# Left-over attention columns split with the first tile, a later product in the retention, row sums of the last down-projection on VectorE

## The chip, the cores and the metric

The kernel runs on one NeuronCore of a Trainium2 chip. A core has five engines with an instruction queue each: TensorE (PE; its weight loads are shown apart as PEld), VectorE (DVE), ScalarE (ACT), GpSimd (POOL) and SyncE (SP), which here issues the DMAs. Each runs its queue in order and waits on semaphores for the others. The metric is the device time in microseconds of one execution; lower is better.

## The reference, cut to what matters

The kernel computes one layer of a hybrid encoder in float32: an input projection, stick-breaking attention beside multi-scale retention, an output projection, and a gated feed-forward block with a causal convolution. Three places matter here.

Attention of the prompt: 8 heads of 64, keys 0 to 2063 (16 meta tokens and 2048 frames), each query reading the keys before it:

```python
z = jnp.einsum('bhqd,bhkd->bhqk', q, k) * (SB_HEAD_DIM ** -0.5)
log_1m = jnp.where(mask, jax.nn.log_sigmoid(-z), 0.0)
later = lax.cumsum(log_1m, axis=z.ndim - 1, reverse=True) - log_1m
a = jnp.where(mask, jnp.exp(jax.nn.log_sigmoid(z) + later), 0.0)
return jnp.einsum('bhqk,bhkd->bhqd', a, v)
```

Retention: the output of each head is normalised by its own root mean square and multiplied by a gate:

```python
ret = _head_norm(ret_o, g_ret_out, RET_HEADS) * jax.nn.silu(r_g)
```

Feed-forward: `u = h @ w_up`, a convolution of width 3 along the tokens, `f = (silu(gate) * val) @ w_down`, the residual sum, and a last RMS norm.

## The kernel before, in words

A float32 product is made of two halves: ACT rounds a tile to its high part and another engine subtracts that from the tile to get the low part; PE then multiplies high by high, high by low and low by high. The profile shows these pairs as `wh`/`wl` and `fh`/`fl` (lines 102 and 103), and as `ahi`/`alo` in the attention (1117 and 1118).

**Attention.** The program runs through the projection and the attention of the sample rows first (to 425 us), then through the prompt's attention (425 to 1275 us). There the work is cut into units: 256 queries (two tiles of 128) by up to 512 keys, for one head. A unit has three stages, written two or three units apart: scores and their sigmoids (L1095 to 1098, ACT L889), with the running products along the keys (DVE scan L899) and their multiplication into the weights on POOL (L905); `t()`, in which PE transposes the weights block by block into two PSUM tiles `tt`, one for each query tile (L1124, L1127), and the helper `evac` splits what is there into `ahi` (ACT) and `alo` (DVE, in0 the PSUM tile, in1 `ahi`); and `av()`, the product with the values (L1157). The PSUM pool of `tt` has two buffers, so that the transposes of the next unit wait until both splits of this one have been read. 2064 keys are 16 blocks of 128 and 16 more; so the last unit of each pair of query tiles and head, 64 units in all, has 16 columns left over (`rem`), which are transposed as two more blocks, one for each query tile, into the first PSUM tile. Such a unit has three splits: the blocks of tile 0, the left-over columns of both, the blocks of tile 1.

**Retention.** `interleave` lays the steps of the retention between those of the attention by estimated PE time. The retention goes through 17 token tiles for each of 4 heads; each has eight steps of projection (`k` 0 to 7, three matmuls `dm` each, L798 to 800), and between them stand the steps of `tail()` of the two tiles before: `prev` and `prev2`. What the table in the loop says for `prev2` is, in order: products with the state, the norm factor `rs` on POOL (L95, L97), `mt` = oc x rs x gate on DVE (L783), and the store of `mt`. The tile `gate` has two buffers; ACT writes it first (L717) when the eight steps of its tile are through, and that buffer is the one which `mt` of two tiles before reads.

**Last down-projection.** The second half of the tokens is multiplied with `w_down` by a Strassen-like scheme of seven products P1, P5, P2, P6, P4, P7, P3, eleven steps (`NH`) each: 77 steps `n` of nine matmuls (three token tiles by three halves, L1816 to 1818). The left operands are quarters of `f`, loaded from DRAM; `sum_part` makes the sums of quarters that P5, P6, P7 and P3 need, 44 in all, on POOL (L1399 to 1405), at steps that the table `when` gives. `split_part` makes `fh` and `fl` two steps ahead, and `part()` goes on with splitting the weights; per step DVE makes one `fl` and one `wl`. `taken` adds a finished product from PSUM into the output tiles `y` (DVE L1732 from PSUM, POOL L1732 from the tile `t`). In the steps n < 4 the last convolution of the up-projection is worked off (DVE L1456 and L1464, POOL L1462), two steps of it for each n.

## Time and profile before

| | |
|---|---|
| time, median of 3 runs | 3021.35 us (3019.08 to 3021.6) |
| the profiled execution's own time | 3019.77 us |
| its span | 3018.0 us, mean granted clock 0.993 |
| busy: PE, PEld | 2920.7 us (97%), 2600.2 us (86%) |
| busy: DVE, ACT, POOL | 2176.0 (72%), 1569.4 (52%), 1648.1 us (55%) |
| DMA | 535.15 MB, mean 177 GB/s |

"Busy" is time in which an engine executes; what a row shows in brackets, as `[2.36 <-DVE alo L1118]`, is the idle time of the engine right before that row and the instruction that ended it. Time outside the span (1.8 us) is start and end of the program.

### The profile page before, as it was taken

Reading aid. Unit: us, or ns where it says so; the run is one execution under the profiler, and the core shown is the slowest. Engines: PE = TensorE matmul, PEld = TensorE weight load, DVE = VectorE, ACT = ScalarE, POOL = GpSimd, SP = SyncE. Lnnn points to the kernel's source line nnn. Section 1 sums busy time; section 2 is a strip of 40 time slices with the busy share of each in tenths; the row PEclk is TensorE's granted clock in tenths of the full one; section 3 lists DMA queues with packets and bytes.
Section 4 is the critical chain, followed back from the end, with each engine's and each line's share of the span. In section 5 each row is a group of like instructions: output and inputs, shape, how many; then the busy total and the mean of one; then the engine's idle time right before and its main releaser. Section 6 shows DMA issues by size and latency. Waiting matters only on the chain. (4 is left out here: it accounts for less than half of the span.)

```text
span 3018.0 us, 48868 instructions
## 1 busy us (share of the span) xinstructions
PE 2920.7 (97%) x16735; PEld 2600.2 (86%) x16735; DVE 2176.0 (72%) x3061; ACT 1569.4 (52%) x3532; POOL 1648.1 (55%) x1826
## 2 busy tenths in 40 slices
PE   7999999999999999999999999999999999999998
PEld 6888688788888878877899998789998879999776
DVE  4331359888888888844348887778888667888897
ACT  5332467777777777643334344454444444444554
POOL 1220368788788878843335565434446343444455
PEclk9999999999999999999999999999999999999999
DMA  6865763443343443258658986655445655444662
GB/s 221 286 213 174 271 195 105 127 133 106 126 147 106 124 138 99 83 205 266 188 180 264 285 278 232 195 168 153 150 149 166 229 187 165 149 149 149 220 220 93
DMA packets 295780, 535.15 MB, mean 177 GB/s; under 512 B 38548, under 2 KB 125972, under 8 KB 283628
## 3 DMA queue, kind: packets, MB, share of 16 engines
q1 hardware_dynamic: 295532, 532.03, 54.2%
q8 instruction: 133, 2.18, 0.3%
q14 instruction: 115, 0.94, 0.1%
HBM read 383.16 MB, written 148.62 MB: 176 GB/s over the span
## 5 line engine op out<-in xcount | busy, mean ns | idle before, releaser
L905 POOL TENSOR_TENSOR sp<-sp,pr 128x272 f32<-128x272 f32 (+7 forms) x453 | 482.5, 1086 | 170.2 <-DVE pr L899 54.8
L103 POOL TENSOR_TENSOR wl<-raw,wh 128x512 fp32r<-128x512 f32 x220 | 325.8, 1482 | 377.6 <-ACT wh L102 358.0
L102 ACT ACTIVATE wh<-raw 128x512 fp32r<-128x512 f32 x561 | 342.6, 623 | 211.6 <-DMA raw<-d_ws 147.0
L1548 PE MATMUL mm<-xs,wl 128*128 128x384 f32 x1232 | 411.5, 334 | 0.0
L1547 PE MATMUL mm<-xs,wh 128*128 128x384 f32 x1232 | 411.5, 334 | 0.0
L1546 PE MATMUL mm<-xs,wh 128*128 128x384 f32 x1232 | 411.5, 334 | 0.0
L899 DVE TENSOR_TENSOR_SCAN pr<-sn,pr 128x513 f32<-128x513 f32 (+2 forms) x320 | 363.1, 1173 | 29.8 <-ACT sn L889 23.8
L1456 DVE SCALAR_TENSOR_TENSOR c<-u,cw,c 128x768 f32<-128x768 f32 (+1 forms) x264 | 343.8, 1302 | 2.5 <-POOL u L1450 1.3
L103 DVE TENSOR_TENSOR wl<-raw,wh 128x512 fp32r<-128x512 f32 x341 | 268.0, 786 | 18.1 <-ACT wh L102 17.6
L1462 POOL TENSOR_TENSOR c<-u,c 128x768 f32<-128x768 f32 (+1 forms) x66 | 116.4, 1764 | 269.7 <-ACT u L1461 264.7
L1118 DVE TENSOR_TENSOR alo<-tt,ahi 128x256 fp32r<-128x256 f32 (+3 forms) x496 | 217.1, 473 | 56.5 <-ACT ahi L1117 55.5
L798 PE MATMUL dm<-wh,xt 128*128 128x512 f32 (+1 forms) x544 | 244.2, 449 | 4.9 <-ACT vtok L459 2.6
L1117 ACT ACTIVATE ahi<-tt 128x256 fp32r<-128x256 f32 (+3 forms) x496 | 194.1, 442 | 91.5 <-DVE alo L1118 66.7
L1546 PEld LDWEIGHTS mm<-xs,wh 128*128 128x128 f32 x1232 | 231.3, 188 | 0.1
L1547 PEld LDWEIGHTS mm<-xs,wh 128*128 128x128 f32 x1232 | 231.3, 188 | 0.1
L1548 PEld LDWEIGHTS mm<-xs,wl 128*128 128x128 f32 x1232 | 231.3, 188 | 0.0
L800 PE MATMUL dm<-wh,xt 128*128 128x512 f32 (+1 forms) x544 | 215.6, 396 | 0.0
L799 PE MATMUL dm<-wl,xt 128*128 128x512 f32 (+1 forms) x544 | 215.1, 395 | 0.0
L889 ACT ACTIVATE sn<-z 128x512 f32<-128x512 f32 (+2 forms) x360 | 169.4, 471 | 80.5 <-PE z L1096 28.1
L1506 PE MATMUL mm<-xt,wh 128*128 128x298 f32 x704 | 204.2, 301 | 0.0
L1505 PE MATMUL mm<-xt,wh 128*128 128x298 f32 x704 | 203.3, 301 | 0.0
L1124 PE MATMUL tt<-ident,sp 128*128 128x128 f32 x1088 | 170.7, 274 | 27.6 <-DVE alo L1118 22.3
(285 smaller groups left out, 8052.0 us busy)
## 6 DMA issues: line engine op xcount, KB each, us to landing
xt<-d_xt SPq DMA_DIRECT2D x68, 1024.0 KB
raw<-in_wup SPq DMA_DIRECT2D x220, 256.0 KB
raw<-d_ws SPq DMA_DIRECT2D x176, 256.0 KB
raw<-in_wdn SPq DMA_DIRECT2D x121, 256.0 KB
d_ws<-raw SPq DMA_DIRECT2D x88, 256.0 KB
d_xt<-xt SPq DMA_DIRECT2D x17, 1024.0 KB
d_f<-c SPq DMA_DIRECT2D x44, 384.0 KB
fr<-d_f SPq DMA_DIRECT2D x44, 384.0 KB
```

What stands on the lines that cost most here:

```text
L102: S.activation(out=hi, in_=raw, func=AF.Copy)
L103: lo_engine.tensor_tensor(out=lo, in0=raw, in1=hi.bitcast(F32), op=ALU.subtract)
L798: PE.matmul(ps[:r], lhsT=xt[:, 0, k, :r], rhs=wh, start=k == 0, stop=False)
L799: PE.matmul(ps[:r], lhsT=xt[:, 0, k, :r], rhs=wl, start=False, stop=False)
L800: PE.matmul(ps[:r], lhsT=xt[:, 1, k, :r], rhs=wh, start=False, stop=k == KD - 1)
L899: V.tensor_tensor_scan(out=pr[:, j, s:n + 1], data0=sn[:, j, s:n + 1], data1=sn[:, j, s:n + 1], initial=1.0 if carry is None else carry[:, ...
L905: G.tensor_tensor(out=sp[:, j, c], in0=sp[:, j, c], in1=pr[:, j, c], op=ALU.mult)
L1118: V.tensor_tensor(out=lo[d], in0=x, in1=hi[d].bitcast(F32), op=ALU.subtract)
L1456: V.scalar_tensor_tensor(out=cvs[e][:, :W], in0=u[:, 2 - y:W + 2 - y], scalar=cw[:, ch, y:y + 1], in1=cvs[e][:, :W], op0=ALU.mult, op1=ALU ...
L1546: PE.matmul(ps, lhsT=wh[:, w], rhs=x[:, 0], start=k == 0, stop=False)
L1547: PE.matmul(ps, lhsT=wh[:, w], rhs=x[:, 1], start=False, stop=False)
L1548: PE.matmul(ps, lhsT=wl[:, w], rhs=x[:, 0], start=False, stop=k == 3)
```

## The change

1. `t()`: the transposed left-over columns of both query tiles are split together with the blocks of tile 0, as one piece of `nb + 2` blocks; so two splits for such a unit in place of three, and `av()` takes the last block's two halves from `src[:, 0, nb:nb + 2]`. 64 splits on ACT and 64 on DVE fall away, and the same columns are covered.
2. Retention: the step of `prev2` with `mt` goes from k = 4 to k = 5, and the one with its store from k = 5 to k = 6.
3. Last down-projection: the sums of quarters go from POOL to DVE, each in the step three before its use; the quarters' buffers are opened at n = 0, on the pool stack's right side, and their loads begin at n = 2 in place of 4; `y11` and `y21` are loaded elsewhere; the convolution goes over ten steps, one piece each; products are taken from k = 3 on. After P6, POOL adds `tmp` into `y12`, `y21` and `y22`; P7 then goes from PSUM straight into `y21` and `y22` by DVE. POOL's adds stay nine. PE's instructions keep their order in the whole program.

```diff
--- before.py
+++ after.py
@@ -798,7 +798,7 @@
                     PE.matmul(ps[:r], lhsT=xt[:, 0, k, :r], rhs=wh, start=k == 0, stop=False)
                     PE.matmul(ps[:r], lhsT=xt[:, 0, k, :r], rhs=wl, start=False, stop=False)
                     PE.matmul(ps[:r], lhsT=xt[:, 1, k, :r], rhs=wh, start=False, stop=k == KD - 1)
-                    for who in {0: (prev,), 1: (prev2,), 2: (prev2,), 4: (prev, prev2), 5: (prev2,), 6: (prev,)}.get(k, ()):
+                    for who in {0: (prev,), 1: (prev2,), 2: (prev2,), 4: (prev,), 5: (prev2,), 6: (prev, prev2)}.get(k, ()):
                         next(who, None)
                     if h + 1 < RH and ((i == 0 and 1 <= k < 7) or (1 <= i <= 2 and k == 4)):
                         part()
@@ -1129,10 +1129,10 @@
                         if u is not None:
                             for x in range(2):
                                 PE.transpose(tp[:, nb + x], u.os[:, 128 * x:128 * x + 128], ident)
-                        if nb > off:
-                            evac((slice(None), j, slice(off, nb)), tp[:, off:nb])
-                        if rem and j == 0:
-                            evac((slice(None), slice(None), nb), tp[:, nb:nb + 2])
+
+                        to = nb + 2 if rem and j == 0 else nb
+                        if to > off:
+                            evac((slice(None), j, slice(off, to)), tp[:, off:to])
                         if u is not None:
                             u.finish(tp[:, nb:nb + 2])
                     yield 220 * nb + (440 if rem else 0)
@@ -1154,7 +1154,8 @@
                         end = self.c == self.nch - 1 and x == len(seq) - 1
                         vs = vt[:, b0 + b, 128 * e:128 * e + 128]
                         for z, src in enumerate((self.hi, self.lo)):
-                            PE.matmul(o[:, :w], lhsT=vs, rhs=src[:, 0:w // 128, b], start=first and z == 0, stop=end and z == 1)
+                            rhs = src[:, 0, b:b + 2] if b == self.nb else src[:, 0:w // 128, b]
+                            PE.matmul(o[:, :w], lhsT=vs, rhs=rhs, start=first and z == 0, stop=end and z == 1)
                         if x % 2 == 1:
                             yield 440
                     if self.c == self.nch - 1:
@@ -1396,13 +1397,13 @@
                 q = {x: t[:, k] for x, t in quarters.items()}
                 name = DOWN_PRODUCTS[j][0]
                 if name == "P5":
-                    G.tensor_tensor(out=q["s"], in0=q["21"], in1=q["22"], op=ALU.add)
+                    V.tensor_tensor(out=q["s"], in0=q["21"], in1=q["22"], op=ALU.add)
                 elif name == "P6":
-                    G.tensor_tensor(out=q["s"], in0=q["s"], in1=q["11"], op=ALU.subtract)
+                    V.tensor_tensor(out=q["s"], in0=q["s"], in1=q["11"], op=ALU.subtract)
                 elif name == "P7":
-                    G.tensor_tensor(out=q["21"], in0=q["11"], in1=q["21"], op=ALU.subtract)
+                    V.tensor_tensor(out=q["21"], in0=q["11"], in1=q["21"], op=ALU.subtract)
                 elif name == "P3":
-                    G.tensor_tensor(out=q["s"], in0=q["12"], in1=q["s"], op=ALU.subtract)
+                    V.tensor_tensor(out=q["s"], in0=q["12"], in1=q["s"], op=ALU.subtract)
 
         def split_part(b, n):
             if n < 7 * NH:
@@ -1713,6 +1714,12 @@
                     if x >= 1:
                         out_of(x - 1)
 
+        def opened_quarters():
+            stb.close()
+            fp = pool(std, "p4fq", 1, "right")
+            for q in ("21", "22", "12", "s"):
+                quarters[q] = fp.tile([128, NH, WB // 2], F32, name=f"f{q}")
+
         def down_fast(opened, b, W, last_conv, gfin):
 
             tiles = blocks[b]
@@ -1773,14 +1780,13 @@
                 elif name == "P6":
                     V.tensor_tensor(out=tmp[x], in0=ps, in1=tmp[x], op=ALU.add)
                     yield
-                    add("12", x, tmp[x], G)
+                    for q in ("12", "21", "22"):
+                        add(q, x, tmp[x], G)
                 elif name == "P4":
                     add("21", x, ps)
                 elif name == "P7":
-                    V.tensor_tensor(out=tmp[x], in0=ps, in1=tmp[x], op=ALU.add)
-                    yield
-                    add("21", x, tmp[x], G)
-                    add("22", x, tmp[x], G)
+                    add("21", x, ps)
+                    add("22", x, ps)
                     yield
                     square("21", x)
                     scaled("21", x)
@@ -1794,18 +1800,10 @@
                     finish(1, x)
                 yield
 
-            loads = [(4 + k, q, k) for k in range(NH) for q in ("21", "22")]
-            loads += [(4 + NH + k, "12", k) for k in range(NH)]
-            loads += [(NH - 2 + x, "y11", x) for x in range(nt)] + [(2 * NH - 4 + x, "y12", x) for x in range(nt)]
-            loads += [(2 * NH - 2 + x, "y22", x) for x in range(nt)] + [(4 * NH + x, "y21", x) for x in range(nt)]
-
-            when = {}
-            for n in range(NH, 2 * NH):
-                when.setdefault(n - 3, []).append(n)
-            at = 2 * NH - 2
-            for n in list(range(3 * NH, 4 * NH)) + list(range(5 * NH, 7 * NH)):
-                when.setdefault(min(int(at), n - 3), []).append(n)
-                at += 1.6
+            loads = [(2 + k, q, k) for k in range(NH) for q in ("21", "22")]
+            loads += [(NH + 4 + k, "12", k) for k in range(NH)]
+            loads += [(NH + x, "y11", x) for x in range(nt)] + [(2 * NH - 4 + x, "y12", x) for x in range(nt)]
+            loads += [(2 * NH - 2 + x, "y22", x) for x in range(nt)] + [(3 * NH + x, "y21", x) for x in range(nt)]
             taking = []
             for j, (name, _) in enumerate(DOWN_PRODUCTS):
                 pss = [pm.tile([128, 512], F32, name="mm", tag="mm") for _ in range(nt)]
@@ -1820,7 +1818,9 @@
                 held = []
                 for k in range(NH):
                     n = j * NH + k
-                    if n == 4:
+                    if n == 0:
+                        opened_quarters()
+                    if n == NH - 1:
                         for _ in last_conv:
                             pass
                         pl = opened()
@@ -1829,8 +1829,7 @@
                             load_y(q[1:], kk)
                         else:
                             load_quarter(b, q, kk, W)
-                    for x in when.get(n, ()):
-                        sum_part(x)
+                    sum_part(n + 3)
                     split_part(b, n + 2)
                     part()
                     ops = (*parts.pop(n), *wts.pop(("e", b, j, k)))
@@ -1839,12 +1838,11 @@
                         continue
                     for x in range(nt):
                         products(x, k, ops)
-                        if not n and x == 0:
+                        if x == n == 0:
                             next(last_conv, None)
-                    if n < 4:
+                    if n < NH - 1:
                         next(last_conv, None)
-                        next(last_conv, None)
-                    for _ in range((k > 0) + (j == 6)):
+                    for _ in range((k > 2) + (j == 6)):
                         if taking:
                             t = taking.pop(0)
                             if next(t, 1) is None:
@@ -1894,10 +1892,6 @@
                     stx.close()
                     p4["xb"] = pool(stb, "p4xb", 1, "right")
                 if fast:
-                    stb.close()
-                    fp = pool(std, "p4fq", 1)
-                    for q in ("21", "22", "12", "s"):
-                        quarters[q] = fp.tile([128, NH, W // 2], F32, name=f"f{q}")
                     return pool(std, "p4y", 3)
                 pl = pool(std, "p4y", 6)
                 if b + 1 == len(blocks):
```

The order on DVE around one such unit of the attention, before (`pr` is the scan of one query tile, `alo` the low half of a split, `mt` the product of the retention, `scm` its masked scores, `ob` the output of a finished head):

```order
L899 SCALAR_TENSOR_TENSOR pr<-sn_2686,pr 128x513 x2
L783 SCALAR_TENSOR_TENSOR mt<-oc,rs,gate 128x128
L1118 TENSOR_TENSOR alo<-tt,ahi 128x256
L1118 TENSOR_TENSOR alo<-tt,ahi 128x2x128
L1118 TENSOR_TENSOR alo<-tt,ahi 128x128
L1173 TENSOR_REDUCE ob<-tt 128x2x64
L754 TENSOR_TENSOR scm<-rs,tri_t 128x128
```

and now:

```order
L899 SCALAR_TENSOR_TENSOR pr<-sn_2686,pr 128x513 x2
L1118 TENSOR_TENSOR alo<-tt,ahi 128x512
L1118 TENSOR_TENSOR alo<-tt,ahi 128x128
L1174 TENSOR_REDUCE ob<-tt 128x2x64
L783 SCALAR_TENSOR_TENSOR mt<-oc,rs,gate 128x128
L754 TENSOR_TENSOR scm<-rs,tri_t 128x128
L899 SCALAR_TENSOR_TENSOR pr<-sn_2687,pr 128x513 x2
```

`mt` stood ahead of the unit's splits and stands behind them, and three `alo` are two.

The order on POOL in the last down-projection, before, from the last piece of the convolution to the last sum (`fs`, `f` are quarters and their sums; `y<-t,y` adds a taken product, `y<-y,gfin` scales an output tile):

```order
L1462 TENSOR_TENSOR c<-u,c 128x768
L1399 TENSOR_TENSOR fs<-f_32487,f_32488 128x384 x11
L1401 TENSOR_TENSOR fs<-fs,f_28785 128x384 x11
...
L1405 TENSOR_TENSOR fs<-f_32489,fs 128x384 x9
L1732 TENSOR_TENSOR y<-t,y 128x512 x4
L1405 TENSOR_TENSOR fs<-f_32489,fs 128x384
L1732 TENSOR_TENSOR y<-t,y 128x512 x2
L1757 TENSOR_TENSOR y<-y,gfin 128x512 x3
L1405 TENSOR_TENSOR fs<-f_32489,fs 128x384
```

and now:

```order
L1463 TENSOR_TENSOR c<-u,c 128x768
L1764 TENSOR_TENSOR y<-y,gfin 128x512 x3
L1739 TENSOR_TENSOR y<-t,y 128x512 x9
L1764 TENSOR_TENSOR y<-y,gfin 128x512 x3
L1751 TENSOR_TENSOR ss<-ss 128x1
```

No sum of quarters is left in POOL's queue; the nine adds stand together.

The order on DVE at the start of the last down-projection, before (`c` are pieces of the convolution):

```order
L103 TENSOR_TENSOR wl<-raw,wh 128x512
L1456 SCALAR_TENSOR_TENSOR c<-u,cw,c 128x768 x2
L103 TENSOR_TENSOR fl<-f_28785,fh 128x384
L103 TENSOR_TENSOR wl<-raw,wh 128x512
L1456 SCALAR_TENSOR_TENSOR c<-u,cw,c 128x768 x2
L103 TENSOR_TENSOR fl<-f_28785,fh 128x384
L103 TENSOR_TENSOR wl<-raw,wh 128x512
L1464 TENSOR_TENSOR c<-c 128x768
```

and now, from the same place on to the first sum:

```order
L1457 SCALAR_TENSOR_TENSOR c<-u,cw,c 128x768 x2
...
L1457 SCALAR_TENSOR_TENSOR c<-u,cw,c 128x768
L103 TENSOR_TENSOR fl<-f_28657,fh 128x384
L103 TENSOR_TENSOR wl<-raw,wh 128x512
L1457 SCALAR_TENSOR_TENSOR c<-u,cw,c 128x768
...
L1465 TENSOR_TENSOR c<-c 128x768
...
L1400 TENSOR_TENSOR fs<-f_32268,f_32269 128x384
L103 TENSOR_TENSOR fl<-f_28657,fh 128x384
L103 TENSOR_TENSOR wl<-raw,wh 128x512
```

The second pair of pieces is taken apart, and one sum stands in each step from there on.

## Rows read from the trace of the kernel before

**Rows 1.** Two stretches of the program: the stretch and its length, then the busy us (and instructions) of PE, PEld, DVE, ACT and POOL, the granted clock, the DMA share and GB/s.

```profile
425.00:1275.00 850.00, 817.45 (x5424) 716.34 (x5423) 741.78 (x1281) 621.09 (x1810) 700.27 (x830) 1.00 0.37 121
...
2826.00:3018.00 192.00, 168.39 (x699) 130.57 (x697) 160.03 (x195) 94.26 (x187) 92.21 (x83) 0.97 0.54 180
```

**Rows 2.** Who waited for whom in 425 to 1275 us: total us, times, longest us.

```profile
ACT ahi L1117 <- DVE alo L1118: 63.1, 63, 4.1
DVE alo L1118 <- ACT ahi L1117: 53.4, 103, 2.0
...
DVE mt L783 <- POOL rs L97: 29.6, 29, 2.7
...
PE tt L1124 <- DVE alo L1118: 20.5, 22, 2.4
```

**Rows 3.** Groups of instructions by line and shape in 425 to 1275 us: number, busy us, mean ns, idle time before them.

```profile
L798 PE MATMUL dm<-wh,xt 128*128 128x512 f32 x414 | 180.9, 437 | 0.0
L1118 DVE TENSOR_TENSOR alo<-tt,ahi 128x256 fp32r<-128x256 f32 x306 | 118.6, 415 | 52.1 <-ACT ahi L1117 51.4
L1118 DVE TENSOR_TENSOR alo<-tt,ahi 128x512 fp32r<-128x512 f32 x116 | 74.5, 674 | 2.2 <-ACT ahi L1117 1.9
L783 DVE SCALAR_TENSOR_TENSOR mt<-oc,rs,gate 128x128 f32<-128x128 f32 x51 | 36.9, 724 | 27.6 <-POOL rs L97 27.6
```

**Rows 4.** The timeline (start, duration, instruction, idle time before it) around one unit with left-over columns: three rows of DVE, one of ACT, one of PE.

```profile
643.83 1.36 DVE L783 SCALAR_TENSOR_TENSOR mt<-oc,rs,gate 128x128 f32<-128x128 f32 x1 [0.38 <-POOL rs L97]
645.12 0.41 DVE L1118 TENSOR_TENSOR alo<-tt,ahi 128x256 fp32r<-128x256 f32 x1
645.98 0.62 DVE L1118 TENSOR_TENSOR alo<-tt,ahi 128x256 fp32r<-128x256 f32 x2 [0.45 <-ACT ahi L1117]
645.56 0.55 ACT L1117 ACTIVATE ahi<-tt 128x256 fp32r<-128x256 f32 x2 [2.75 <-DVE alo L1118]
646.55 0.63 PE L1124 MATMUL tt<-ident,sp 128*128 128x128 f32 x4 [1.35 <-DVE alo L1118]
```

**Rows 5.** The timeline around a stall of PE elsewhere: two rows of DVE, one of PE.

```profile
548.60 0.35 DVE L783 SCALAR_TENSOR_TENSOR mt<-oc,rs,gate 128x128 f32<-128x128 f32 x1 [1.31 <-POOL rs L97]
550.84 0.60 DVE L1118 TENSOR_TENSOR alo<-tt,ahi 128x256 fp32r<-128x256 f32 x2
551.39 0.85 PE L1124 MATMUL tt<-ident,sp 128*128 128x128 f32 x6 [1.00 <-DVE alo L1118]
```

**Rows 6.** ACT's split of a quarter in two neighbouring steps of the last down-projection.

```profile
2962.82 0.53 ACT L102 ACTIVATE fh<-f 128x384 fp32r<-128x384 f32 x1 [1.01 <-issue]
2964.88 0.53 ACT L102 ACTIVATE fh<-f 128x384 fp32r<-128x384 f32 x1 [1.01 <-issue]
```

**Rows 7.** Seven stretches of the last down-projection, columns as in Rows 1.

```profile
2826.00:2847.00 21.00, 14.32 (x56) 9.51 (x55) 17.66 (x28) 12.05 (x22) 5.68 (x6) 1.00 0.63 216
2847.00:2875.00 28.00, 28.00 (x124) 22.98 (x123) 24.62 (x31) 14.69 (x28) 13.32 (x12) 1.00 0.99 336
2875.00:2899.00 24.00, 21.99 (x87) 15.42 (x87) 24.00 (x27) 11.23 (x22) 15.75 (x12) 1.00 0.83 297
...
2920.00:2931.00 11.00, 9.42 (x38) 6.47 (x37) 10.94 (x10) 6.38 (x14) 9.13 (x7) 1.00 0.34 107
2931.00:2959.00 28.00, 27.74 (x122) 22.42 (x120) 28.00 (x30) 14.50 (x28) 21.12 (x15) 1.00 0.45 142
2959.00:2994.00 35.00, 34.98 (x153) 28.66 (x153) 30.67 (x40) 18.22 (x40) 13.08 (x9) 1.00 0.23 66
2994.00:3007.00 13.00, 8.29 (x26) 6.06 (x25) 4.86 (x8) 3.40 (x6) 6.64 (x12) 0.74 0.33 122
```

**Rows 8.** DVE at the start of the last down-projection, with the convolution's pieces.

```profile
2836.78 2.07 DVE L1456 SCALAR_TENSOR_TENSOR c<-u,cw,c 128x768 f32<-128x768 f32 x2
...
2844.82 0.96 DVE L1464 TENSOR_TENSOR c<-c 128x768 f32<-128x768 f32 x1 [1.85 <-POOL c L1462]
```

**Rows 9.** DVE's splits with POOL quiet (2898 us) and with POOL at its sums (2926 us).

```profile
2898.49 0.55 DVE L103 TENSOR_TENSOR fl<-f,fh 128x384 fp32r<-128x384 f32 x1
2898.96 0.68 DVE L103 TENSOR_TENSOR wl<-raw,wh 128x512 fp32r<-128x512 f32 x1
...
2925.47 1.37 DVE L103 TENSOR_TENSOR fl<-fs,fh 128x384 fp32r<-128x384 f32 x1
2926.76 1.49 DVE L103 TENSOR_TENSOR wl<-raw,wh 128x512 fp32r<-128x512 f32 x1
```

**Rows 10.** POOL's sums for P6, POOL's last sum, and PE at the end.

```profile
2874.42 14.90 POOL L1401 TENSOR_TENSOR fs<-fs,f 128x384 f32<-128x384 f32 x11
2996.16 1.00 POOL L1405 TENSOR_TENSOR fs<-f,fs 128x384 f32<-128x384 f32 x1
3000.91 0.79 PE L1816 MATMUL mm<-wh,fh 128*128 128x512 f32 x1 [3.93 <-ACT fh L102]
```

**Rows 11.** Groups by line and shape in 2825 to 3018 us, as in Rows 3: one of PE, three of POOL.

```profile
L1816 PE MATMUL mm<-wh,fh 128*128 128x512 f32 x231 | 91.6, 397 | 5.3 <-ACT fh L102 5.3
L1405 POOL TENSOR_TENSOR fs<-f,fs 128x384 f32<-128x384 f32 x11 | 14.8, 1376 | 0.0
L1732 POOL TENSOR_TENSOR y<-t,y 128x512 f32<-128x512 f32 x9 | 13.7, 1540 | 30.7 <-DVE t L1780 22.4 <-DVE t L1774 8.3
L1399 POOL TENSOR_TENSOR fs<-f,f 128x384 f32<-128x384 f32 x11 | 12.8, 1162 | 16.9 <-DMA f<-d_f 16.9
```

## The prediction

> **What bounds the kernel now.** I read the busy times by stretch first [rows 1]. The two stretches that the change touches differ. In the attention (850 us) PE is busy 817.45 us, so 32.6 us of it are open; DVE is busy 741.78 us, or 87%, and POOL 700.27. In the last down-projection (192 us) PE is open for 23.6 us, DVE is busy 160.03 and POOL only 92.21. Ahead of 2826 us the change touches nothing but the attention and the retention beside it. PE sets the pace in both; the question is which of its open microseconds end with something that the change shortens.
>
> For the attention the waits say it [rows 2]. PE's largest wait is the transpose `tt` for `alo`: 20.5 us in 22 times. That is the PSUM tile that is not yet read. Behind it stand ACT waiting for `alo` (63.1 us, 63 times), DVE waiting for `ahi` (53.4, 103 times) and `mt` waiting for `rs` (29.6, 29 times). The timeline shows how they hang together [rows 4]: `mt` waits 0.38 us for POOL and runs 1.36; the first `alo` of the unit begins only at 645.12; ACT has been waiting 2.75 us for it; then the last `alo` waits 0.45 for ACT, and PE, idle for 1.35 us, goes on at 646.55. The second place [rows 5] has no left-over columns: `mt` waits 1.31 us, `alo` comes late by that, PE loses 1.00.
>
> For the last down-projection I set matmuls against time. ACT's rows stand 2.06 us apart [rows 6], so nine matmuls take 2.06 and one 0.229. Each stretch's count times 0.229, taken from its length, is what is lost there [rows 7]: 8.2 us in 2826 to 2847 (56 matmuls, 12.8 of 21), none to 2875, 4.1 to 2899 (87), 2.3 in 2920 to 2931 (38), 0.1 to 2959, none to 2994 (153 x 0.229 = 35.0), 7.05 in 2994 to 3007 (26). Together 21.8 us.
>
> **The change part by part.** Two splits for three: two pieces of 256 cost DVE 2 x 415 ns, one of 512 674 [rows 3]. That is 156 ns, x 64 = 10 us of DVE, and the third split's idle 0.45 us x 64 = 29 us more of its time [rows 4]. None of it is on the path by itself, since DVE's work hides beside PE; it counts where PE waits for `alo`. Merged, the first split begins later, behind two more transposes, and ends 0.26 us later; but the first PSUM tile was held for the second of the three splits anyway, so its release is no later than before. ACT's second wait, for DVE to be done with the first piece, goes.
>
> `mt` one step later: 414 `dm` triples lie in 850 us [rows 3], so a step is 2.05 us, and the mean wait of `mt` is 29.6 / 29 = 1.02 [rows 2]. Most of the waits go; those of 2.1 to 2.7 stay in part. So DVE gets back up to some 28 us of standing. The store of `mt` moves by as much and stays one step behind it on SP's queue, so that nothing behind it is held longer. POOL's `rs` does not become earlier; only DVE no longer stands for it.
>
> What PE gets of this: the 20.5 us, and a little more, since a matmul that lasts 0.397 us [rows 11] is followed after 0.229 when nothing waits, so each stall costs up to 0.17 beyond the idle shown, 22 x 0.17 = 3.7. Of these 24 us both causes together cover most, but behind DVE the scans remain (DVE would still have some 732 us of work in 850). I take 17. The ends: nothing, if each stall has a second cause that comes up at once (the next is PE's own order and POOL's products); and 33 us plus 5 of restarts, if all of PE's open time goes.
>
> The start of the down-projection: a pair of pieces of the convolution is 2.07 us on DVE [rows 8], beside 0.55 + 0.68 of splits, 3.3 a step where PE needs 2.06. Now most steps hold one piece, 0.55 + 0.68 + 1.04 = 2.27, less the overlap of neighbouring rows (0.55 long, but 0.47 apart [rows 9]), about 2.05. One pair still stands. I take 2.5 of the 8.2 us (one pair's excess of 1.0, and most of the 1.85 for POOL's piece, which now has steps in between).
>
> The sums on DVE: no row shows one. The nearest is `fl`, the same shape, two inputs from SBUF: 0.55 with POOL quiet, 1.37 beside POOL [rows 9]; POOL itself takes 1.16 to 1.38 [rows 11]. I take 0.55, because POOL has no sums left to run beside it: 0.55 + 0.68 + 0.55 = 1.78, below 2.06. So 44 sums cost PE nothing. The upper end, 1.38, makes a step 2.61, or 2.37 with three overlaps of 0.08, and 44 x 0.31 = 14 us of loss. Below nothing it cannot go.
>
> What leaves with POOL's sums: beside its 14.90 us of P6 sums [rows 10] DVE's splits took 1.37 and 1.49, that is 2.8 a step instead of 1.2, and PE lost 4.1 us there and, beside P7's, 2.3 and 0.1 [rows 7]. These 6.5 go. At the end `fh` waited for the last sum, issued behind POOL's adds at 2996.16, and PE lost 3.93 in one piece [rows 10], then ran at 0.74 of its clock [rows 7], that is partly at 1.2 in place of 2.4 GHz, having stood idle before; of the 7.05 us I take 6.5. What is new: nine adds of 1.54 us stand together after P6 [rows 10, 11], 13.9 us in which DVE's two splits need some 2.7 a step, five steps with 0.65 too much, 3.3 us, less what the two steps of lead take up; I take 1.5. P7 costs DVE six adds for three before, two or three us in steps that have room. The quarters come two steps sooner; DMA is full at 0.99 from 2847 to 2875 [rows 7] and POOL's first sums waited 16.9 us for it [rows 11]. On DVE such a wait would hold `fl`; six steps lie between load and use, 12 us, and I take nothing for it.
>
> Sum: 2.5 + 6.5 + 6.5 - 1.5 = 14 for the down-projection, 17 for the attention, 31. The profiled execution took 3019.77, 1.8 more than its span and 1.6 less than the median; from it 31 give 2988.8, from the median 2990.4. I say 2989.
>
> **The rivals.** *The attention gains nothing.* PE's 817 us and POOL's 700 would set the pace, and a removed stall would be waited for elsewhere, in `alo` behind the scans. For it: DVE would still be 732 / 850 = 86% busy, POOL 82%. Against it: the waits of PE name `alo`, and both rows that I followed end in pieces that go. 3021 - 14 = 3007.
>
> *The sums are as dear on DVE as on POOL.* 1.38 each: loss 14, so the down-projection gains nothing, 3021 - 17 = 3004. Against it: `fl` at 0.55. The same time comes out if DVE waits for quarters, about 14 us in all. The Trainium skill ("Perfetto Trace Analysis", Optimizing Scalar/DVE Operations) speaks for this one: VectorE and GpSimd share a read port, so shifting operations between the two might not help. The rows at 0.55 and 1.37 agree that the two disturb each other, yet they also show that the disturbance ends when POOL is quiet, which it becomes.
>
> *All stalls of the attention go*, 38 us, and the down-projection's 14 beside: 3021 - 52 = 2969, or some 2973 if part of the restarts stays.
>
> *Slower: the gate.* `mt` reads the `gate` buffer that ACT refills at the end of step 7. From step 4 there were three steps, 6.1 us; from step 5 there are two, 4.1. If DVE lags behind ACT by more, ACT stands at L717 and with it the sigmoids and `ahi` queued behind, for which POOL and PE wait. The longest wait of ACT for DVE is 4.1 us [rows 2], so it decides just there. With 51 products in the stretch [rows 3], 2 us each and half of it on PE: 51 us lost, less 14: 3058; with 1 us each 3032, which I take as its time. Against it: the mean lag is far smaller, 63.1 / 63 = 1.0 us [rows 2].
>
> *Nothing in sum*, gains of one part eaten by the other: 3021.
>
> **How the numbers follow.** My forecast 0.50, own range 2976 to 3002 (attention 7 to 27, down-projection 12 to 18). No gain in the attention 0.16, dear sums 0.12, all stalls gone 0.10, the gate 0.06, nothing 0.06. The range 2973 to 3010 holds the forecast and most of the first three rivals. 0.2%, about 6 us, is what a measurement of this kernel can tell from no change: faster is the forecast (0.50), all stalls gone (0.10) and the two at 3004 and 3007 (0.28), less 0.01, so 0.87; the same is the last case, 0.06; slower is the gate with that 0.01, 0.07.
>
> **What would show it.** The two splits: rows of `alo` 128x512 rise by about 64, PE's wait for `alo` falls from 20.5 to below 8, DVE's for `ahi` to about 25. `mt` waits for `rs` less than 8 us in all. The attention ends by 1258 rather than 1275. In the down-projection DVE's sums take 0.55, `fl` stays at 0.55 nearly everywhere, PE's wait of 3.93 at the end is gone, and it lasts about 178 us. I am wrong if ACT's `gate` waits for `mt` some 50 times, if the sums take over 0.9 us, or if PE's waits in the attention carry another name with the same sum.

## The result, and the profile after

| | before | changed |
|---|---|---|
| time, median | 3020.64 us (4 runs) | 2988.86 us (4 runs, 2986.61 to 2991.24) |
| ratio | | 0.9895, 95% interval 0.9878 to 0.9913 |
| span of the profiled execution | 3018.0 us | 2989.5 us |

The changed kernel is 32 us faster (interval 26 to 37). The forecast was 2989, the range 2973 to 3010.

The attention's stretch first, with the columns of [rows 1]; the last down-projection now begins 13.5 us earlier, at 2814.8, and comes further down.

```profile
425.00:1275.00 850.00, 827.38 (x5526) 729.66 (x5525) 757.45 (x1240) 626.45 (x1766) 721.50 (x846) 1.00 0.38 123
```

In the same 850 us PE does 102 more matmuls, DVE is busy 16 us more and POOL 21 us more than in [rows 1]: more of the same work falls into the window. The first and the last attention product with `ahi` start at these times, before (L1157) and in the changed kernel (L1158):

```profile
L1157 PE MATMUL o<-ahi,vt x640: 220/280/415, 434.3 to 1289.7; 128*128 128x256 f32 x144, 128*128 128x128 f32 x16
L1158 PE MATMUL o<-ahi,vt x640: 220/280/415, 434.0 to 1271.5; 128*128 128x256 f32 x144, 128*128 128x128 f32 x16
```

The attention is 18 us shorter by them: 837.5 us from first to last, 855.4 before.

Who waited for whom, over nearly the same work as in [rows 2] (425 to 1262 us: 5443 matmuls, 5424 before):

```profile
DVE alo L1118 <- ACT ahi L1117: 50.0, 70, 2.2
...
PE tt L1124 <- DVE alo L1118: 8.5, 11, 1.3
...
DVE mt L783 <- POOL rs L97: 6.0, 11, 0.7
```

ACT's wait for `alo`, the longest of all before (63.1 us), is no longer among the rows of this window; one of 1.9 us comes behind it. `mt` stands 6.0 us for 29.6, and PE's wait for the PSUM tile is 8.5 for 20.5. One row has hardly moved: DVE still waits 50.0 us for `ahi`, 53.4 before, in fewer and longer pieces. The groups, against [rows 3]:

```profile
L1118 DVE TENSOR_TENSOR alo<-tt,ahi 128x512 fp32r<-128x512 f32 x181 | 118.7, 676 | 32.2 <-ACT ahi L1117 31.6
...
L1118 DVE TENSOR_TENSOR alo<-tt,ahi 128x256 fp32r<-128x256 f32 x181 | 70.8, 412 | 18.7 <-ACT ahi L1117 18.4
L783 DVE SCALAR_TENSOR_TENSOR mt<-oc,rs,gate 128x128 f32<-128x128 f32 x52 | 40.0, 769 | 5.4 <-POOL rs L97 5.4
```

There are 65 more rows of 128x512 and 125 fewer of 128x256. The idle time that stood before the small ones (52.1 us) is now divided, and 31.6 of it stand before the large ones. The timeline of DVE at a unit with left-over columns shows why; it answers to [rows 4]:

```profile
636.18 0.89 DVE L1118 TENSOR_TENSOR alo<-tt,ahi 128x512 fp32r<-128x512 f32 x2 [0.25 <-ACT ahi L1117]
636.99 0.41 DVE L1174 TENSOR_REDUCE ob<-tt 128x128 f32<-128x256 f32 x1
637.32 0.64 DVE L783 SCALAR_TENSOR_TENSOR mt<-oc,rs,gate 128x128 f32<-128x128 f32 x1
```

DVE now comes to the splits early and waits for ACT; it came late before, and ACT waited. `mt` follows with no wait.

The last down-projection in stretches of the same lengths, from its first matmul on, with the columns of [rows 7]:

```profile
2814.80:2835.80 21.00, 17.52 (x71) 12.88 (x72) 19.21 (x29) 13.46 (x25) 5.71 (x6) 1.00 0.84 286
2835.80:2863.80 28.00, 28.00 (x124) 22.99 (x123) 24.14 (x46) 15.66 (x31) 0.00 (x0) 1.00 0.94 324
2863.80:2887.80 24.00, 24.00 (x107) 19.69 (x106) 19.77 (x36) 11.91 (x24) 0.00 (x0) 1.00 0.94 327
...
2919.80:2947.80 28.00, 27.17 (x118) 21.68 (x117) 28.00 (x39) 13.05 (x26) 13.47 (x9) 1.00 0.42 114
2947.80:2981.40 33.60, 32.77 (x141) 25.74 (x139) 29.18 (x48) 18.08 (x40) 9.46 (x15) 1.00 0.17 60
```

By the same count of matmuls times 0.229 us, 4.7 us are lost at the start (71 x 0.229 = 16.3 of 21), none from 2835.8 to 2919.8, where POOL is nearly idle, 1.0 beside POOL's adds and 1.3 at the end. From the first matmul to the start of the last it takes 166.4 us (2814.78 to 2981.21), where it took 180.9 (2828.33 to 3009.25); without any stall it would be 158.4. So 22.5 us of stalls have become 8.0. By the gaps, which here are the distances between the starts of neighbouring matmuls beyond 0.229, they were 7.3 in the first 30 us, 7.3 in the middle and 7.5 at the end; they are 4.9, 1.4 and 1.6. The groups of DVE there have the sums:

```profile
L1404 DVE TENSOR_TENSOR f<-f,f 128x384 f32<-128x384 f32 x11 | 7.0, 640 | 0.0
L1406 DVE TENSOR_TENSOR fs<-f,fs 128x384 f32<-128x384 f32 x11 | 6.8, 618 | 0.0
L1402 DVE TENSOR_TENSOR fs<-fs,f 128x384 f32<-128x384 f32 x11 | 6.0, 548 | 0.0
L1400 DVE TENSOR_TENSOR fs<-f,f 128x384 f32<-128x384 f32 x11 | 6.0, 548 | 0.0
```

0.55 us each where POOL is quiet, as `fl` took it, against 1.16 to 1.40 on POOL. Where POOL is not quiet, it looks like this; the first row is POOL, the next four DVE, the last PE:

```profile
2919.00 14.27 POOL L1739 TENSOR_TENSOR y<-t,y 128x512 f32<-128x512 f32 x9 [14.91 <-DVE t L1781]
2928.90 1.64 DVE L1404 TENSOR_TENSOR f<-f,f 128x384 f32<-128x384 f32 x1
2930.47 1.65 DVE L103 TENSOR_TENSOR fl<-f,fh 128x384 fp32r<-128x384 f32 x1
...
2933.74 0.54 DVE L1404 TENSOR_TENSOR f<-f,f 128x384 f32<-128x384 f32 x1
2934.21 0.54 DVE L103 TENSOR_TENSOR fl<-f,fh 128x384 fp32r<-128x384 f32 x1
2932.18 0.51 PE L1816 MATMUL mm<-wh,fl 128*128 128x512 f32 x1 [0.55 <-DVE fl L103]
```

The sum and `fl` take 1.64 beside POOL's adds and 0.54 right after them. The lead of two steps carries DVE through most of the 14 us; PE stands only twice.

### The profile page after: what moved, and what is told of

Same layout as the page of the kernel before. It is cut to its first block, busy times and chain, and to the rows that moved or that the text cites. A ratio compares the mean times of both kernels' runs of the same rounds, so it can differ in the third digit from the quotient of the medians.

```text
span 2989.5 us, 48849 instructions
## 1 busy us (share of the span) xinstructions
PE 2912.0 (97%) x16735; PEld 2599.7 (87%) x16735; DVE 2172.5 (73%) x3044; ACT 1567.0 (52%) x3468; POOL 1605.9 (54%) x1782
## 5 line engine op out<-in xcount | busy, mean ns | idle before, releaser
L103 DVE TENSOR_TENSOR wl<-raw,wh 128x512 fp32r<-128x512 f32 x341 | 249.5, 732 | 21.6 <-ACT wh L102 21.1
L1118 DVE TENSOR_TENSOR alo<-tt,ahi 128x512 fp32r<-128x512 f32 (+3 forms) x432 | 207.2, 519 | 52.8 <-ACT ahi L1117 51.9
L1671 PE MATMUL mm<-wh,fl 128*128 128x512 f32 (+1 forms) x484 | 192.0, 397 | 3.9 <-DVE fl L103 3.7
L1669 PE MATMUL mm<-wh,fh 128*128 128x512 f32 (+1 forms) x484 | 190.5, 394 | 4.9 <-ACT fh L102 4.9
```

What stands on the lines that cost most here:

```text
L103: lo_engine.tensor_tensor(out=lo, in0=raw, in1=hi.bitcast(F32), op=ALU.subtract)
L1669: PE.matmul(pss[x][:r], lhsT=fh[:, c], rhs=wh, start=k == 0, stop=False)
L1671: PE.matmul(pss[x][:r], lhsT=fl[:, c], rhs=wh, start=False, stop=k == NF - 1)
```

## The experiments

All differences are against the kernel before on the same chip, with the 95% interval.

**The four parts alone.** `e1_merge` has the first of these two edits of the kernel before (with the `rhs` in `av()` that belongs to it), `e2_mt` the second, `e3_merge_mt` both; `e4_down` has all of the change but these two.

```diff
-                            evac((slice(None), j, slice(off, nb)), tp[:, off:nb])
-                        if rem and j == 0:
-                            evac((slice(None), slice(None), nb), tp[:, nb:nb + 2])
+                            evac((slice(None), j, slice(off, to)), tp[:, off:to])
...
-... 4: (prev, prev2), 5: (prev2,), 6: (prev,)}.get(k, ()):
+... 4: (prev,), 5: (prev2,), 6: (prev, prev2)}.get(k, ()):
```

> The kernel before with the two merged splits alone; `mt` and the last down-projection as before. The kernel before takes about 3020.6 us, the changed one gained some 13 to 14 us ahead of 2812 us by its trace. Theory A (both edits of the attention shorten the same chain on DVE, each about half): 6 to 9 us faster, 3012 to 3015; rows of `alo` 128x512 rise by 64, ACT's wait for `alo` falls from 63 us to below 30. Rival B (the standing of `mt` alone holds PE): within 2 us, 3019 to 3022. Rival C (the merged splits give nearly all): 3006 to 3009.

> The kernel before with `mt` (and its store) one step later alone. Theory A: 6 to 9 us faster, 3012 to 3015; DVE's wait for `rs` falls from 29.6 to below 8 us. Rival B (it gives all of the attention's gain): 3006 to 3009. Rival C (it gives nothing, since DVE then stands in the splits instead): 3019 to 3022. The gate rival: slower, with waits of ACT's `gate` for `mt`.

> Both edits of the attention, the last down-projection as before. Theory: the two gains add up to the 13 to 14 us of the trace, 3006 to 3008, and the two parts of the whole change do not touch each other. Rival: they overlap with the down-projection's part (other loads, another pool), and this one gives 9 us or less.

> The kernel before with the edits of the last down-projection alone. Theory (my sum of 14; the trace shows the stretch from the first to the last matmul 14.5 us shorter): 3005 to 3008. Rival (part of that gain is the quieter attention's, by a shifted DMA load): 9 us or less, above 3011.

Measured: the splits alone 0.9973 (0.9961 to 0.9984), that is 8 us; `mt` alone 0.9967 (0.9955 to 0.998), 10 us; both 0.9931 (0.9918 to 0.9945), 21 us; the down-projection alone 0.9945 (0.9932 to 0.9957), 17 us. Theory A holds: neither edit gives it all, and both theories that said so fall. The sum of the two single gains, 18, agrees with the 21 of both within the intervals. The 21 are more than the 13 to 14 expected, which were read at the end of one trace of the changed kernel (below). And 21 + 17 = 38 stands against 32 for all; its interval goes to 37, so nothing is shown to be lost between the parts, though a few us may be.

The traces give the attention by itself, from the start of its first product to that of its last:

| kernel | us |
|---|---|
| before; `e4_down` | 855.4; 856.3 |
| `e1_merge` | 851.1 |
| `e2_mt` | 849.6 |
| `e3_merge_mt`, the changed kernel twice, `e6` to `e11` | 837.3 to 839.5 |
| `e5_dummy` | 843.0 |

By this count the splits alone give 4 to 5 us, `mt` alone 6 to 7, both 16 to 19. That is more than their sum, as if each edit gained by the other; with one trace for each single edit it is a hint, and the medians can't tell it.

What one edit does without the other is read from the waits (425 to 1262 us). With the splits alone:

```profile
DVE mt L783 <- POOL rs L97: 44.4, 32, 3.2
DVE alo L1118 <- ACT ahi L1117: 38.4, 62, 1.9
...
PE tt L1124 <- DVE alo L1118: 18.4, 20, 2.4
```

The freed time of DVE went in part into the next wait: `mt` now stands 44.4 us for `rs`, 27.1 in this window before. PE's wait for the tile is 18.4 for 20.5, so that row holds 2 us of the gain; where PE won the rest was not followed. With `mt` alone:

```profile
DVE alo L1118 <- ACT ahi L1117: 63.4, 114, 2.1
ACT ahi L1117 <- DVE alo L1118: 59.7, 62, 4.0
...
PE tt L1124 <- DVE alo L1118: 12.0, 19, 1.6
...
DVE mt L783 <- POOL rs L97: 5.1, 8, 1.4
```

Here DVE and ACT go on waiting for each other as before, and only the stalls behind `mt` have gone. Both together bring PE's row to 8.8 us.

**Time saved or wait removed?** The merging saves DVE 0.16 us and ACT 0.18 in each unit, and takes away ACT's wait. `e5_dummy` gives the engine time back and leaves the wait out:

```diff
                             evac((slice(None), j, slice(off, to)), tp[:, off:to])
+                            if rem and j == 0:
+                                S.activation(out=hi[:, 1, 3], in_=hi[:, 0, nb].bitcast(F32), func=AF.Copy)
+                                V.tensor_tensor(out=lo[:, 1, 3], in0=tp[:, nb], in1=hi[:, 0, nb].bitcast(F32), op=ALU.subtract)
```

> The changed kernel (about 2989), with one more ACT copy (128x128, about 0.29 us) and one more DVE subtraction (128x128, about 0.28 us) in each of the 64 units with left-over columns, right behind the merged split; neither makes ACT wait for DVE. They write blocks that nothing reads. That puts back more engine time than the merging saved (0.16 and 0.18 us). Theory (the merging helps because ACT's second split had to wait for DVE's first): it keeps its gain, 2988 to 2993. Rival (it helps by the engine time saved on DVE and ACT): the 8 us are given back, 2996 to 2999.

Measured: 2990.91, ratio 0.9897 (0.9883 to 0.9911). With the 8 us given back it would be 0.9922, outside the interval: most of the gain stays, and the wait is what counted most. By the trace not all of it stays: the attention takes 843.0 us, where nine others with both edits take 837.3 to 839.5. So the added work costs 4 to 6 of the some 11 us that the merging gives beside the later `mt` (849.6 to 838). It is more work than the merging saved, and part of its cost is a new wait, since the added subtraction reads the PSUM tile too (425 to 1262 us):

```profile
PE tt L1124 <- DVE alo L1138: 2.8, 4, 1.5
```

In the program's waits ACT's second split of such a unit, which reads the same PSUM tile as the first, waits for DVE's first; with one split for each tile there is no second reading. That it is the shared tile which asks for the wait is read from there and was not tried by itself.

**The sums on POOL or on DVE.** `e6_sums_pool` leaves all else of the change and puts the 44 sums back:

```diff
-                    V.tensor_tensor(out=q["s"], in0=q["21"], in1=q["22"], op=ALU.add)
+                    G.tensor_tensor(out=q["s"], in0=q["21"], in1=q["22"], op=ALU.add)
...
```

> The changed kernel with the 44 sums on POOL again, still one in each step, three ahead of their use. Theory (a POOL sum beside DVE's splits makes both dear: 1.37 for 0.55): DVE's two splits take 2.3 to 2.7 us in such a step, PE needs 2.06, so 44 x 0.25 to 0.6 = 11 to 27 us slower, 3000 to 3016. Rival (only the bunching of the sums and their place in POOL's queue did harm; spread out they are hidden): 2987 to 2992.

Measured: 3001.0, ratio 0.9935 (0.9922 to 0.9947), 12 us slower than the changed kernel. The down-projection took 179.4 us (2809.81 to 2989.25) for 166.4. So one sum for each step of the program is not enough on POOL. POOL, DVE and PE in its trace:

```profile
2935.37 12.18 POOL L1404 TENSOR_TENSOR f<-f,f 128x384 f32<-128x384 f32 x9
2939.88 1.37 DVE L103 TENSOR_TENSOR fl<-f,fh 128x384 fp32r<-128x384 f32 x1
2941.17 1.50 DVE L103 TENSOR_TENSOR wl<-raw,wh 128x512 fp32r<-128x512 f32 x1
2942.60 1.37 DVE L103 TENSOR_TENSOR fl<-f,fh 128x384 fp32r<-128x384 f32 x1
2941.31 0.50 PE L1816 MATMUL mm<-wh,fl 128*128 128x512 f32 x1 [0.38 <-DVE fl L103]
2944.02 0.51 PE L1816 MATMUL mm<-wh,fl 128*128 128x512 f32 x1 [0.37 <-DVE fl L103]
```

They did not stay spread out: behind the three adds POOL had fallen back, and made nine sums in a row. Beside them a step takes 2.71 us (2941.31 to 2944.02) where PE needs 2.06. Where sums did stay apart, the rival was right: seven of P5's run one by one between 2836 and 2851 us. A POOL row and two of DVE:

```profile
2842.10 1.23 POOL L1400 TENSOR_TENSOR fs<-f,f 128x384 f32<-128x384 f32 x1 [1.42 <-DMA f<-d_f]
2842.38 1.37 DVE L103 TENSOR_TENSOR fl<-fs,fh 128x384 fp32r<-128x384 f32 x1
2843.67 0.68 DVE L103 TENSOR_TENSOR wl<-raw,wh 128x512 fp32r<-128x512 f32 x1
```

Mostly only one of DVE's two splits in a step is dear there, and PE's matmuls start no more than 0.24 us apart. So this run shows what sums cost that bunch up behind POOL's other work; a kernel that keeps all of them apart on POOL was not tried.

A sum on POOL and a split on DVE disturb each other. This is the rule of the Trainium skill ("SBUF — State Buffer", Who interferes with whom): a VectorE instruction with two inputs from SBUF contends with a GpSimd instruction that reads SBUF. The traces agree, 0.55 for 1.37 and 0.54 for 1.64. The caution of the Trainium skill ("Perfetto Trace Analysis", Optimizing Scalar/DVE Operations), that a shift between these two engines might not help, did not decide here: the sum is cheaper on DVE, and with POOL quiet the splits beside it become cheap as well.

**How much room DVE has.** `e7_sum_twice` doubles the disputed cost:

```diff
+                if name in ("P5", "P6", "P7", "P3"):
+                    V.tensor_tensor(out=spare[0], in0=quarters["11"][:, k], in1=quarters["11"][:, 0], op=ALU.subtract)
```

> The changed kernel with a second DVE subtraction of the same shape beside each of the 44 sums, into a spare tile that nothing reads. Theory (a sum is 0.47 us of DVE's pace and DVE has room): a step is 0.47 + 0.60 + 2 x 0.47 = 2.01, below PE's 2.06; up to 3 us slower where taken products are added too, 2989 to 2993. Rival (DVE is already at the edge): 44 x 0.47 = 21 us slower, about 3010.

Measured: 2997.7, ratio 0.9917 (0.9904 to 0.993), by the ratios 7 us above the changed kernel; the stretch took 175.9 us (2813.45 to 2989.36) for 166.4. Neither number was right. Where POOL is quiet the doubled sums cost nothing: from 45 to 116 us after the first matmul no gap is left. The price is paid mostly where POOL runs, and then again in the clock. Rows of PE:

```profile
2932.22 0.51 PE L1819 MATMUL mm<-wh,fl 128*128 128x512 f32 x1 [1.78 <-DVE fl L103]
...
2973.64 0.50 PE L1819 MATMUL mm<-wh,fl 128*128 128x512 f32 x1 [2.75 <-DVE fl L103]
...
2975.17 0.63 PE L1818 MATMUL mm<-wl,fh 128*128 128x512 f32 x1
2975.59 0.63 PE L1819 MATMUL mm<-wh,fl 128*128 128x512 f32 x1
```

After a stall of 1.78 and one of 2.75 us the matmuls follow each other in 0.42 for 0.229, with the granted clock at 0.76 in 2974 to 2981, that is partly at 1.2 GHz; each such piece costs some 1.5 us beside its stall.

**A still later `mt`.** `e8_mt6` moves it and its store again:

```diff
-... 4: (prev,), 5: (prev2,), 6: (prev, prev2)}.get(k, ()):
+... 4: (prev,), 6: (prev, prev2), 7: (prev2,)}.get(k, ()):
```

> The changed kernel with `mt` one step later again (k = 6) and its store at k = 7: one step, 2.05 us, between `mt` and the `gate` that refills its buffer, for two. Theory (the mean lag of DVE is about 1 us; 6.0 us of waits for `rs` are left): 2986 to 2991. The gate rival: ACT waits for `mt` at the `gate`, 10 to 50 times, and the time is 2996 or more.

Measured: 2984.96, ratio 0.9884 (0.9869 to 0.9899), no difference from the changed kernel that could be told. The waits:

```profile
ACT gate L717 <- DVE mt L783: 2.8, 3, 1.9
...
DVE mt L783 <- POOL rs L97: 0.5, 1, 0.5
```

With one step between them the `gate` does wait for `mt`, three times, 2.8 us in all. With two steps, in the changed kernel, no such row is listed.

**Loads, convolution, and the two together.** `e10_late_loads` and `e11_conv_pairs` each undo one edit of the down-projection; `e9_best` is `e8_mt6` without the extra piece of the convolution at n = 0; `e12_after_again` is the changed kernel, on the same chip.

```diff
-            loads = [(2 + k, q, k) for k in range(NH) for q in ("21", "22")]
+            loads = [(4 + k, q, k) for k in range(NH) for q in ("21", "22")]
```

> The changed kernel with the loads of the quarters 21 and 22 at n = 4 + k again. Theory (four steps, 8 us, are enough): within 3 us of the changed kernel, 2986 to 2992, no wait of DVE's sums for `f`. Rival (DMA is full there, and a sum on DVE that waits holds `fl`): 3 to 10 us slower, with waits of the first sums for a DMA.

```diff
-                    if n < NH - 1:
-                        next(last_conv, None)
+                    if n < 4:
+                        next(last_conv, None)
+                        next(last_conv, None)
```

> The changed kernel with the convolution's steps two for each n < 4, as before. Theory (my term of 2.5 us): 1.5 to 3.5 us more time from the first to the last matmul of the last down-projection than the 166.4 us of the changed kernel; in all 2990 to 2993. Rival (the start is bound by the first split and by DMA, not by these pieces): no difference.

```diff
-                        if x == n == 0:
-                            next(last_conv, None)
```

> The changed kernel (about 2989) with `mt` at k = 6, its store at k = 7, and no extra piece of the convolution at n = 0, so that no two pieces stand together on DVE. In the trace of the changed kernel the pair left over costs PE 1.5 us and the step behind it 0.9; the later `mt` gave nothing that could be told apart. Theory: 1 to 3 us faster than the changed kernel, 2984 to 2988; its stall of 1.5 us some 8 us after the first matmul is gone. Rival (the convolution's end only comes later and holds a load): the stall stands elsewhere, no gain.

> The changed kernel once more, beside the other three on the same chip. Expected: 2989, between 2985 and 2993; it bounds what can be told apart here.

Measured, ratio and time from the first matmul to the start of the last:

| | ratio | us |
|---|---|---|
| late loads | 0.9895 (0.988 to 0.9909) | 166.4 |
| pairs of pieces | 0.9899 (0.9885 to 0.9914) | 169.0 |
| no extra piece, later `mt` | 0.9887 (0.987 to 0.9903) | 165.1 |
| changed, again | 0.9889 (0.9875 to 0.9904) | 166.2 |

The loads' two steps are worth nothing. The spreading of the convolution is worth 2.8 us in the stretch, as its theory had it, though the whole time can't tell that. Taking the extra piece out gives 1.1 us there and no better time: 2985.39 against 2985.54 for the changed kernel beside it. No version here is shown to beat the changed kernel. The stall that I had laid to the pair of pieces is still there, at 8 us:

```profile
2816.95 0.96 DVE L1465 TENSOR_TENSOR c<-c 128x768 f32<-128x768 f32 x1 [1.40 <-POOL c L1463]
2817.82 0.55 DVE L103 TENSOR_TENSOR fl<-f,fh 128x384 fp32r<-128x384 f32 x1
```

`fl` stands behind a piece of the convolution that waits 1.40 us for POOL. Only the 0.9 behind it was the pair's, and that is gone.

## Why the prediction was right, point by point

**The time** was right, and so were its two halves: 14 us for the last down-projection, where its stretch became 14.5 shorter; 17 for the attention, which became 18 shorter. (I had written of an end at 1275 that goes to 1258; 1275 was the edge of my window, and the last product started at 1289.7.) Of these 18 there were 13.5 at the first matmul of the last down-projection; in the repetition 15.6 (2828.33 to 2812.74). Nothing is shown to be given back on the way: the stretch between, which no edit reaches, took 1538.6 us before, 1543.3 in the changed kernel, 1538.9 in its repetition, and 1534.3 to 1543.3 over all fourteen traces. How the 17 came about was near, too: PE's open time in the attention fell by 12.6 us (34.5 to 21.9), its busy time by 5.3 (820.9 to 815.6), where I had up to 3.7 for restarts; that the 5.3 are restarts is not shown. How much of it PE would get was a guess within bounds, and its closeness is in part luck.

**The merged splits** were right in effect and wrong in one step. "The third split's idle 0.45 us x 64 = 29 us more of its time" did not come: DVE's wait for `ahi` is 50.0 us, where I had said about 25. DVE, come free sooner, waits for ACT before the first split instead. What the merging gave is the end of ACT's wait, which I had named last and without a price; `e5_dummy`, which puts back more engine time than the merging saved, keeps at least half of the gain by its trace and nearly all by its time, so the engine time that I did price was the smaller part.

**The later `mt`** was right: 6.0 us of waits, where I said less than 8. PE's wait for the tile, 8.5, ended just above the 8 that I gave.

**The start of the down-projection**: 2.5 us taken, 2.4 by the gaps (7.3 to 4.9; my 8.2 began at 2826, before the first matmul), 2.8 by undoing it. The 1.85 us for POOL's piece are gone. A wait of the same kind for the piece before it, which I had not named, is still there, 1.40 us. **The sums**: 0.55 was right where POOL is quiet, 0.62 to 0.64 on average where it runs in part, and with that the "dear sums" fell; `fl`, which I expected at 0.55 nearly everywhere, took 0.65 and 0.69 on average (44 and 33 of them). **What leaves with POOL's sums**: 6.5 taken, none lost in the calm stretches; **the nine adds**: 1.5 taken, 1.4 measured in the gaps. **The end**: 6.5 of 7.05 taken, 5.9 gone by the gaps. What is left there is new, and it is on ACT:

```profile
2973.82 0.72 ACT L1756 ACTIVATE y<-y,rs 128x512 f32<-128x512 f32 x1 [0.74 <-POOL rs L97]
2974.45 0.51 ACT L102 ACTIVATE fh<-fs 128x384 fp32r<-128x384 f32 x1
```

`fh` stands behind the scaling of an output tile that waits 0.74 us for POOL's norm factor, and PE waits 0.67 for that `fh` (at 2975.01). I had counted POOL's queue at the end and not ACT's.

**The rivals.** "The attention gains nothing" fell by `e3_merge_mt`, 21 us. "All stalls go" fell: PE's 8.5 us remain, and some 22 us of its time stay open. **The gate** fell with its point of decision: not even with half the margin does it hold ACT for more than 2.8 us.

## What to carry to other kernels

Two engines that take turns at one PSUM tile can wait for each other at every turn, as ACT did here 63 times for 1.0 us; one reading of each, though larger, was better than two, and most of what it gave was the wait and not the work saved. A short operation between two SBUF tiles that is moved from POOL to DVE can pay twice, by its own duration and by what it no longer does to DVE's other work, as long as DVE's step stays under PE's and the few POOL instructions left are bunched where DVE has a lead. Seven sums of `e6_sums_pool` suggest that one left on POOL is hidden too while it stays alone in its step. Price an edit by the wait that it removes, and ask which engine will wait next: freed time of DVE went in part into its next wait until that one was removed too.

## What the runs showed of the hardware

- A DVE sum of two SBUF tiles, 128x384 in float32, took 0.54 to 0.55 us with POOL idle and 1.64 beside POOL's adds; `wl` 128x512 took 0.68 and 1.78. An instruction with one of its two inputs from PSUM was not touched: in the kernel before, two of 128x512 took 1.28 us together between a `wl` of 1.78 and an `fl` of 1.27; the 24 of that shape at L1739 of the changed kernel took 0.68 each:

```profile
2981.32 1.78 DVE L103 TENSOR_TENSOR wl<-raw,wh 128x512 fp32r<-128x512 f32 x1
2983.02 1.28 DVE L1780 TENSOR_TENSOR t<-mm,t 128x512 f32<-128x512 f32 x2
2984.22 1.27 DVE L103 TENSOR_TENSOR fl<-fs,fh 128x384 fp32r<-128x384 f32 x1
```

- A stall of PE can cost 1.3 to 2.3 us more than it lasts, by the slower clock behind it: 1.3 after 1.43 us in `e6_sums_pool`, 1.5 after 1.78 and after 2.75 in `e7_sum_twice`, 2.0 after 3.93 in the kernel before, and, at the start, 2.3 after 1.36 in `e10_late_loads`; not seen in the changed kernel after 1.34 and 0.55. The length of the stall alone does not tell it.
- Single traces of the same code agreed within about 2 us in the attention and in the last down-projection, but differed by up to 9 us (1534.3 to 1543.3) in the long stretch between. A few us of the whole time can't be told from one execution.
